# Hybrid decoder block on one core: the first sixteen ada_w blocks staged at once, the small constants issued by GpSimd

## The chip, the cores and the metric

The kernel runs on one core of a Trainium2 chip. The metric is the time of one execution in microseconds (us), as the device counts it; lower is better. Before the change the median of three runs is 2619.75 us.

## What is computed

One decoder layer over x (2048 tokens by 1024 features, float32). The parts that matter here stand at its start:

```python
c_act = jax.nn.silu(c)
ada = c_act @ ada_w[l] + ada_b[l]          # ada_w: 1024 x 6144
sh_a, sc_a, gt_a, sh_m, sc_m, gt_m = jnp.split(ada, 6)
h = rms_norm(x, pre_norm_mix[l]) * (1.0 + sc_a) + sh_a
y = hybrid_mixer(h, ...)                    # its first step is h @ w_in
x = x + gt_a * rms_norm(y, post_norm_mix[l])
h = rms_norm(x, pre_norm_mlp[l]) * (1.0 + sc_m) + sh_m
y = jnp.square(jax.nn.relu(h @ w_up[l])) @ w_down[l]
x = x + gt_m * rms_norm(y, post_norm_mlp[l])
```

The mixer joins four heads of chunked gated linear attention and four heads of rotary differential attention, and is followed by a squared-ReLU MLP. Nothing of h, and so nothing of the projections, can be formed before the scale `sc_a` and the shift `sh_a` are known.

## The kernel before

The kernel is one long program for the five engines and the DMA queues, written with pools and tiles. A scheduler orders each engine's instructions, and each engine then runs its own list strictly in that order. Matmul operands are split into a high and a low float32r half, so that a product is three matmuls. The program's stages are: the start (ada vectors, the first normalisation), the input projections and the gated linear attention, the differential attention, the output projection, the MLP.

The start goes like this. `ada_chunk(j)` (from L352) forms `c_act @ ada_w` for 1024 columns, number j of six: for each of the eight blocks of 128 rows, SyncE (SP) asks for a 128x1024 float32 block `adaraw` (512 KB, L357) and VectorE (DVE) multiplies it by a column of `ca` (the activated c) and adds it to `adacc`, at L359 for the first block and L361 for the other seven. The tile `adaraw` has the tag `wraw` with three buffers, so a fourth block is asked for when the first has been used. `ada_cols(j)` (L365) then sums `adacc` over its partitions with eight one-column matmuls by `ones` (L369, PSUM tile `adaps`), and L370 adds the sums to `cols`, which held the bias `ada_b`.

The top of the program (from L430) runs j=1 (the scale) for three blocks, then `load_consts()`, twelve small transfers issued by SP (L100 to L111), then the other five blocks. `make_a1` (L386) makes the multiplier `prem`. j=0 (the shift) follows in the same way; after its third block `load_x(0)` asks for the first 512 tokens of x, four tiles `nx` of 128x1024. `load_norm` squares each on ScalarE (ACT, L140, tile `njunk`, sums in `nss`), `rsqrt_col` (L120 to L129, tiles `nry`, `nrv`, `nrw`, `nrr`) makes the root, L145 scales the four tiles on ACT. `modulate` transposes them on TensorE (PE, L155, `ntr`), and ACT applies multiplier and shift at L157 (`nhf`); from these come the operands `hThi` and `hTlo` (L158, L160) of `hT[0]`. The low-rank gate (`lrps` L513 and L514, `zps` L519) and the projections (`projn`, L502 to L504) come next.

A DMA's landing is counted on a semaphore. SP's transfers go round eight of them, so a ninth is not issued before the first of the eight ahead of it has landed; GpSimd (POOL) has eight of its own.

Of the kernel before, what the change touches and what calls it, by code (L numbers as in the profile page):

```python
# [9 lines left out]
F32 = mybir.dt.float32  # L10
# [9 lines left out]
P = 128  # L20
S = 2048
D = 1024
NK = D // P
# [26 lines left out]
def tile_hybrid_block(  # L50
# [3 lines left out]
    nc = tc.nc  # L54
# [35 lines left out]
    cols = const.tile([P, 48], F32, name="cols")  # L90
    prem = const.tile([P, 2, NK], F32, name="prem")
    postm = const.tile([P, 2, NK], F32, name="postm")
    gnc = const.tile([P, 2], F32, name="gnc")
    gbc = const.tile([P, 2], F32, name="gbc")
    ivf = const.tile([P, 1], F32, name="ivf")
    gw2 = const.tile([32, 2, P], F32, name="gw2")
    lamt = const.tile([P, 4, 64], F32, name="lamt")

    def load_consts():
        nc.sync.dma_start(cols, ada_b)  # L100
        nc.sync.dma_start(prem[:, 0, :], pre_mix)
        nc.sync.dma_start(prem[:, 1, :], pre_mlp)
        nc.sync.dma_start(postm[:, 0, :], post_mix)
        nc.sync.dma_start(postm[:, 1, :], post_mlp)
        nc.sync.dma_start(gnc[:, 0:1], gla_norm)
        nc.sync.dma_start(gnc[:, 1:2], diff_norm)
        nc.sync.dma_start(gbc, gate_b)
        nc.sync.dma_start(ivf, inv_freq)
        nc.sync.dma_start(gw2[0:16], gate_w)
        nc.sync.dma_start(gw2[16:32], gate_w)  # L110
        nc.sync.dma_start(lamt, lams.partition_broadcast(P))  # L111

    neglam = const.tile([P, 1], F32, name="neglam")

# [17 lines left out]
    def load_norm(src, xp, slots, on_act=False):  # L132

        xts = []
        ss = xp.tile([P, 4], F32, tag="nss", name="nss", bufs=2)
        for i in range(4):
            xt = xp.tile([P, D], F32, tag=slots[i][0], name="nx", bufs=slots[i][1])
            nc.sync.dma_start(xt, src[i])
            junk = xp.tile([P, D], BF16, tag="njunk", name="njunk", bufs=1)
            nc.scalar.activation(junk, xt, AF.Square, accum_out=ss[:, i:i + 1])  # L140
            xts.append(xt)
        r = rsqrt_col(xp, ss, 4, 1.0 / D, "nr")
        for i in range(4):
            if on_act:
                nc.scalar.activation(xts[i], xts[i], AF.Copy, scale=r[:, i:i + 1])  # L145
            else:
                nc.vector.tensor_scalar(xts[i], xts[i], r[:, i:i + 1], None, op0=ALU.mult)
        return xts
# [157 lines left out]
    sb = c0.enter_context(tc.tile_pool(name="p0", bufs=2, side="left"))  # L306
    sg = cG.enter_context(tc.tile_pool(name="p0g", bufs=2, side="right"))
# [3 lines left out]
    def ps_proj(name):  # L311
        return pp.tile([P, 512], F32, tag="A", name=name, bufs=2)
# [36 lines left out]
            nc.gpsimd.dma_start(ropeS[t][1], sn)  # L349
        tc.keep_in_program_order(nc.scalar.preload_act_table_set("natural_log_exp_and_others"))  # L350

    def ada_chunk(j, acc=None):  # L352
        if acc is None:
            acc = sb.tile([P, D], F32, tag="adacc", name="adacc", bufs=1)
        for k in range(NK):
            raw = sb.tile([P, D], F32, tag="wraw", name="adaraw", bufs=3)
            nc.sync.dma_start(raw, ada_w[k * P:(k + 1) * P, j * D:(j + 1) * D])  # L357
            if k == 0:
                nc.vector.tensor_scalar(acc, raw, ca[:, 0:1], None, op0=ALU.mult)  # L359
            else:  # L360
                nc.vector.scalar_tensor_tensor(acc, raw, ca[:, k:k + 1], acc, op0=ALU.mult, op1=ALU.add)  # L361
            yield
        return acc

    def ada_cols(j, acc=None):  # L365
        acc = yield from ada_chunk(j, acc)
        ps = ps_proj("adaps")
        for b in range(NK):
            nc.tensor.matmul(ps[:, b:b + 1], acc[:, b * P:(b + 1) * P], ones[:, 0:1], start=True, stop=True)  # L369
        nc.vector.tensor_tensor(cols[:, j * NK:(j + 1) * NK], cols[:, j * NK:(j + 1) * NK], ps[:, 0:NK], op=ALU.add)  # L370
# [13 lines left out]
    def make_a1(i, j):  # L384

        nc.vector.scalar_tensor_tensor(prem[:, i, :], cols[:, j * NK:(j + 1) * NK], 1.0, prem[:, i, :],  # L386
                                       op0=ALU.add, op1=ALU.mult)
# [8 lines left out]
    def run(g, n=None):  # L396

        while n is None or n > 0:
            if next(g, run) is run:
                return False  # L400
            n = None if n is None else n - 1
        return True
# [4 lines left out]
    def load_x(t):  # L407
        return load_norm([x[t * 512 + i * P:t * 512 + (i + 1) * P, :] for i in range(4)], sg, NX[t % 2], t == 0)
# [18 lines left out]
            wlo += [wl[:, k, :] for k in range(4)]  # L427
        return whi, wlo

    sc_a = ada_cols(1)  # L430
    run(sc_a, 3)
    load_consts()
    run(sc_a)
    make_a1(0, 1)
    sh_a = ada_cols(0, sb.tile([P, 4, 256], F32, tag="whi", name="adacc", bufs=3).rearrange("p a b -> p (a b)"))
    run(sh_a, 3)
    xts = load_x(0)
    run(sh_a)
    norm_in(0, xts, "CBDCBDCB")

# [406 lines left out]
    for k in range(NK):  # L847
        run(at, WL)
        raw = sw.tile([P, D], F32, tag="wx", name="woraw", bufs=3)
# [197 lines left out]
    wraw = {}  # L1047
# [119 lines left out]
    for s, (g, c, wi, p) in enumerate(usteps):  # L1167
        i = WORD[wi]
# [22 lines left out]
        whi, wlo = wsp.pop((p, i))  # L1191
# [207 lines left out]
    for s in range(nd - TAIL):  # L1399
        if s + AHEAD < nd:  # L1400
            ready_ops[s + AHEAD] = down_ops(*dsteps[s + AHEAD])
        i, p, gs = dsteps[s]
# [98 lines left out]
```

## Time and profile before

| what | value |
|---|---|
| median of 3 runs | 2619.75 us (2618.13 to 2629.93) |
| the profiled execution's own time | 2620.44 us |
| its span, first to last instruction | 2618.7 us |
| granted TensorE clock, mean share of full | 0.982 |
| PE busy, by matmuls | 2482.6 us (95%) |
| DVE busy | 1595.4 us (61%) |
| ACT busy | 1154.8 us (44%) |
| POOL busy | 435.5 us (17%) |
| DMA moved | 491.63 MB, 188 GB/s on average |

Busy shares are averages over stages with different limits. The profile's times run from the first instruction of the span; 1.7 us of the execution's own time lie outside the span.

### The profile page before, as it was taken

The page shows a single profiled execution, that of the slowest core. Times are in us where ns is not written, and L with a number is a line of the kernel's source. Part 1 is how long each engine was busy: PE and PEld are TensorE (multiplying, and loading weights), DVE is VectorE, ACT ScalarE, POOL GpSimd, SP SyncE. Part 2 cuts the span into 40 slices and gives each one's busy share as a digit, 9 for nine tenths or more (in the row PEclk, how much of TensorE's full clock was granted, in tenths as well). Part 3 has the DMA queues.
Part 4 walks back from the last instruction along what each step waited for, and adds up shares of the span by engine and source line. Part 5 has one row for each costly group of instructions (what it writes and reads, how often), then busy time and mean ns, then how long its engine had stood idle before and what let it go on. Part 6 is the DMA issues. An engine that isn't in the chain of part 4 may idle for free.

```text
span 2618.7 us, 35437 instructions
## 1 busy us (share of the span) xinstructions
PE 2482.6 (95%) x12532; PEld 2043.2 (78%) x12532; DVE 1595.4 (61%) x3111; ACT 1154.8 (44%) x2185; POOL 435.5 (17%) x642
## 2 busy tenths in 40 slices
PE   3999999999998899999999999999999999999998
PEld 2887787987787787787877878788888888788886
DVE  5545765247764766766568666866665435443756
ACT  3351224323444655565546454655454324222444
POOL 1211332102320113223002231121121000100000
PEclk9999999999999899999999999999999999999999
DMA  6354552344744756565376564654447857755856
GB/s 235 107 193 137 170 196 77 125 131 155 224 155 142 227 173 207 186 201 187 109 261 234 194 238 141 225 190 144 139 151 258 289 189 234 268 197 162 282 168 208
DMA packets 219898, 491.63 MB, mean 188 GB/s; under 512 B 25872, under 2 KB 79936, under 8 KB 218176
## 3 DMA queue, kind: packets, MB, share of 16 engines
q1 hardware_dynamic: 171504, 329.33, 39.8%
q0 software_dynamic: 48208, 159.95, 16.3%
q8 instruction: 101, 1.65, 0.3%
q14 instruction: 85, 0.70, 0.1%
HBM read 329.79 MB, written 159.39 MB: 187 GB/s over the span
## 4 chain that ended last, share of the span: by engine, by line
PE 33%; issue 20%; DMA 5%; POOL 5%; DVE 3%; ACT 2%; SPq 0%; POOLq 0%; DVEq 0%; ACTq 0%
PE dn L1361 6%; PE dn L1363 6%; PE dn L1362 6%; PE O L252 3%; PE S L209 3%; PE Y L873 1%; PE Y L875 1%; POOL uS L1121 1%; PE Y L874 1%; POOL uS L1152 1%; PE PT L248 1%; DMA mx<-mixS 1%; PE upY L1195 1%; PE upY L1194 1%; PE upY L1193 1%
## 5 line engine op out<-in xcount | busy, mean ns | idle before, releaser
L1361 PE MATMUL dn<-dnhi,uhi 128*128 128x512 f32 x880 | 344.2, 391 | 4.8 <-DVE du L1339 4.7
L1363 PE MATMUL dn<-dnhi,ulo 128*128 128x512 f32 x880 | 343.8, 391 | 0.1
L1362 PE MATMUL dn<-dnlo,uhi 128*128 128x512 f32 x880 | 343.8, 391 | 0.0
L1285 ACT CAST uhi<-us 128x1024 fp32r<-128x1024 f32 (+1 forms) x126 | 118.7, 944 | 352.6 <-PE dn L1362 325.8
L1287 DVE TENSOR_TENSOR ulo<-us,uhi 128x1024 fp32r<-128x1024 f32 (+1 forms) x126 | 137.0, 1087 | 152.6 <-ACT uhi L1285 149.9
L209 PE MATMUL S<-K,q 128*128 128x512 f32 (+3 forms) x640 | 193.9, 402 | 14.2 <-DVE P L214 7.5
L488 PE MATMUL projt<-hThi,whi 128*128 128x512 f32 x512 | 206.3, 403 | 0.6 <-DVE cols L370 0.3
L489 PE MATMUL projt<-hTlo,whi 128*128 128x512 f32 x512 | 205.9, 402 | 0.0
L490 PE MATMUL projt<-hThi,wlo 128*128 128x512 f32 x512 | 201.8, 394 | 2.1 <-DVE wlo L425 2.1
L1361 PEld LDWEIGHTS dn<-dnhi,uhi 128*128 128x128 f32 x880 | 165.7, 188 | 41.0 <-issue 5.1
L1363 PEld LDWEIGHTS dn<-dnhi,ulo 128*128 128x128 f32 x880 | 165.7, 188 | 35.7 <-DVE ulo L1287 0.6
L1362 PEld LDWEIGHTS dn<-dnlo,uhi 128*128 128x128 f32 x880 | 165.7, 188 | 35.1
L227 ACT ACTIVATE P<-P,nm 128x128 f32<-128x128 f32 (+15 forms) x128 | 153.8, 1203 | 65.2 <-DVE nm L217 59.7
L1075 ACT CAST wuhi<-wA 128x512 fp32r<-128x512 f32 x160 | 99.1, 619 | 162.7 <-PE upV L1194 67.2
L252 PEld LDWEIGHTS O<-V,PTs 128*128 128x128 f32 x1088 | 136.5, 193 | 33.4 <-ACT PTs L250 26.6
L252 PE MATMUL O<-V,PTs 128*128 128x128 f32 x1088 | 154.7, 285 | 7.3 <-ACT PTs L250 3.5
L1195 PE MATMUL upY<-hhi,wulo 128*128 128x512 f32 x384 | 151.0, 393 | 1.5 <-DVE wulo L1076 1.5
L1193 PE MATMUL upY<-hhi,wuhi 128*128 128x512 f32 x384 | 150.9, 393 | 0.0
L1194 PE MATMUL upY<-hlo,wuhi 128*128 128x512 f32 x384 | 150.9, 393 | 0.0
L502 PE MATMUL projn<-whi,hThi 128*128 128x256 f32 x512 | 147.2, 288 | 3.8 <-DVE cols L370 2.3
L209 PEld LDWEIGHTS S<-K,q 128*128 128x128 f32 x640 | 111.7, 197 | 48.8 <-DVE P L214 21.9
L503 PE MATMUL projn<-wlo,hThi 128*128 128x256 f32 x512 | 146.7, 287 | 0.0
(321 smaller groups left out, 5759.9 us busy)
## 6 DMA issues: line engine op xcount, KB each, us to landing
us<-uS SPq DMA_DIRECT2D x94, 512.0 KB, 4.5
wA<-in_w_up_dram SPq DMA_DIRECT2D x128, 256.0 KB, 3.0
uS<-t POOLq DMA_DIRECT2D x128, 256.0 KB, 3.2
adaraw<-in_ada_w_dram SPq DMA_DIRECT2D x48, 512.0 KB, 4.4
wraw<-in_w_in_dram SPq DMA_DIRECT2D x48, 512.0 KB, 4.5
uS<-c POOLq DMA_DIRECT2D x96, 256.0 KB, 3.0
K<-kS SPq DMA_DIRECT2D x40, 512.0 KB, 4.6
wds<-in_w_down_dram SPq DMA_DIRECT2D x78, 256.0 KB, 4.3
```

What stands on the lines that cost most here:

```text
L209: nc.tensor.matmul(ps[:, :wd], qt[:, m, hl, qs], Kc[ci][:, m, :wd], start=(hl == 0), stop=(hl == 1))
L227: nc.scalar.activation(Ps[m][:, :width], Ps[m][:, :width], AF.Exp, scale=-1.0, bias=nms[m][:, t:t + 1], accum_out=sums[:, 0, m:m + 1])
L252: nc.tensor.matmul(outs[t, h][:, j, :], pt[:, kb % 4, :], Vc[g][:, kb % 4, :], start=(kb == 0), stop=(kb == nb - 1))
L488: nc.tensor.matmul(ps, whi[k][:, cs], hi[:, k, :], start=(k == 0), stop=False)
L489: nc.tensor.matmul(ps, whi[k][:, cs], lo[:, k, :], start=False, stop=False)
L490: nc.tensor.matmul(ps, wlo[k][:, cs], hi[:, k, :], start=False, stop=(k == NK - 1))
L1193: nc.tensor.matmul(ps, whi[:, k, :], hi[:, k, :], start=(first and k == 0), stop=False, skip_group_check=not first)
L1194: nc.tensor.matmul(ps, whi[:, k, :], lo[:, k, :], start=False, stop=False, skip_group_check=not first)
L1195: nc.tensor.matmul(ps, wlo[:, k, :], hi[:, k, :], start=False, stop=(k == 3), skip_group_check=not first)
L1361: nc.tensor.matmul(banks[t], uhi[:, tk], whi, start=first, stop=False, skip_group_check=on)
L1362: nc.tensor.matmul(banks[t], uhi[:, tk], wlo, start=False, stop=False, skip_group_check=on)
L1363: nc.tensor.matmul(banks[t], ulo[:, tk], whi, start=False, stop=last, skip_group_check=on)
```

## The change

Five edits go together. The twelve constants are issued by POOL instead of SP. A new `ada_stage(j)` asks for all eight blocks of one j at once, into tiles `adast` that take the buffers later used for `hThi` and `hTlo` (two buffers each, four blocks to a buffer). The order of SP's requests is then: eight blocks of j=1, the four tiles of x, eight blocks of j=0. `load_norm` is split, so that the normalisation of x is a function of its own, `norm_rows`, with the same operations. `ada_chunk` and `ada_cols` take the staged blocks, where there are any. The other four j are loaded as before.

```diff
     def load_consts():
-        nc.sync.dma_start(cols, ada_b)
-        nc.sync.dma_start(prem[:, 0, :], pre_mix)
...
-        nc.sync.dma_start(lamt, lams.partition_broadcast(P))
+        nc.gpsimd.dma_start(cols, ada_b)
+        nc.gpsimd.dma_start(prem[:, 0, :], pre_mix)
...
+        nc.gpsimd.dma_start(lamt, lams.partition_broadcast(P))
...
-    def ada_chunk(j, acc=None):
+    def ada_stage(j):
+
+        raws = []
+        for tag in ("hThi", "hTlo"):
+            st = sb.tile([P, NK, 512], F32, tag=tag, name="adast", bufs=2).rearrange("p (r a) b -> p r (a b)", a=2)
+            for r in range(4):
+                k = len(raws)
+                nc.sync.dma_start(st[:, r, :], ada_w[k * P:(k + 1) * P, j * D:(j + 1) * D])
+                raws.append(st[:, r, :])
+        return raws
+
+    def ada_chunk(j, acc=None, raws=None):
...
-            raw = sb.tile([P, D], F32, tag="wraw", name="adaraw", bufs=3)
-            nc.sync.dma_start(raw, ada_w[k * P:(k + 1) * P, j * D:(j + 1) * D])
+            if raws is None:
+                raw = sb.tile([P, D], F32, tag="wraw", name="adaraw", bufs=3)
+                nc.sync.dma_start(raw, ada_w[k * P:(k + 1) * P, j * D:(j + 1) * D])
+            else:
+                raw = raws[k]
...
-    sc_a = ada_cols(1)
-    run(sc_a, 3)
     load_consts()
-    run(sc_a)
+    sc_raw = ada_stage(1)
+    x0 = [sg.tile([P, D], F32, tag="nx", name="nx", bufs=4) for _ in range(4)]
+    for i in range(4):
+        nc.sync.dma_start(x0[i], x[i * P:(i + 1) * P, :])
+    sh_raw = ada_stage(0)
+    run(ada_cols(1, raws=sc_raw))
     make_a1(0, 1)
-    sh_a = ada_cols(0, sb.tile([P, 4, 256], F32, tag="whi", name="adacc", bufs=3).rearrange("p a b -> p (a b)"))
+    sh_a = ada_cols(0, sb.tile([P, 4, 256], F32, tag="whi", name="adacc", bufs=3).rearrange("p a b -> p (a b)"), sh_raw)
     run(sh_a, 3)
-    xts = load_x(0)
+    xts = norm_rows(x0, sg, True)
     run(sh_a)
     norm_in(0, xts, "CBDCBDCB")
```

On SP's queue before, from the second of the two `gnc` constants to the first loads of the input weights (`wraw`; `lraw` is the gate's weight):

```order
L106 DMA gnc<-in_diff_norm_dram 128x1
L107 DMA gbc<-in_gate_b_dram 128x2
L108 DMA ivf<-in_inv_freq_dram 128x1
L109 DMA gw_125<-in_gate_w_dram 16x256
L110 DMA gw_125<-in_gate_w_dram 16x256
L111 DMA lamt<-in_lams_dram 128x256
L357 DMA adaraw<-in_ada_w_dram 128x1024 x8
L138 DMA nx<-in_x_dram 128x1024 x4
L357 DMA adaraw<-in_ada_w_dram 128x1024 x5
```

Ahead of these stand `ccol` (the vector c), three blocks and the first six constants. On SP's queue now, from its start, with what each request waits for (DMAHW0 to DMAHW7 are the eight semaphores of SP's transfers):

```order
L89 DMA ccol<-in_c_dram 128x8
L363 DMA adast<-in_ada_w_dram 128x1024 x7
L363 DMA adast<-in_ada_w_dram 128x1024 [waits DMAHW0_49]
L452 DMA nx<-in_x_dram 128x1024 [waits DMAHW1_49]
L452 DMA nx<-in_x_dram 128x1024 [waits DMAHW2_49]
L452 DMA nx<-in_x_dram 128x1024 [waits DMAHW3_49]
L452 DMA nx<-in_x_dram 128x1024 [waits DMAHW4_49]
L363 DMA adast<-in_ada_w_dram 128x1024 [waits DMAHW5_49]
L363 DMA adast<-in_ada_w_dram 128x1024 [waits DMAHW6_49]
```

The constants are gone from between the blocks, the waits on DVE are gone too, and x stands behind eight blocks instead of eleven; six more blocks of j=0 follow the last row.

On DVE before, from the second block of j=1 to the root of x (`nrr`):

```order
L361 SCALAR_TENSOR_TENSOR adacc<-adaraw,ca,adacc 128x1024 x2
L472 TENSOR_SCALAR gnc<-gnc 128x1
L361 SCALAR_TENSOR_TENSOR adacc<-adaraw,ca,adacc 128x1024 x5
L370 TENSOR_TENSOR cols<-cols,adaps 128x8
L359 TENSOR_SCALAR adacc<-adaraw,ca 128x1024
L386 SCALAR_TENSOR_TENSOR prem<-cols,prem 128x8
L361 SCALAR_TENSOR_TENSOR adacc<-adaraw,ca,adacc 128x1024 x2
L123 TENSOR_SCALAR nrv<-nss 128x4
L361 SCALAR_TENSOR_TENSOR adacc<-adaraw,ca,adacc 128x1024
L126 TENSOR_TENSOR nrw<-nry 128x4
L127 SCALAR_TENSOR_TENSOR nrw<-nrw,nrv 128x4
L129 SCALAR_TENSOR_TENSOR nrr<-nrw,nry 128x4
```

And on DVE now, from the same place to the end of the shift's blocks:

```order
L379 SCALAR_TENSOR_TENSOR adacc<-adast,ca,adacc 128x1024 x5
L493 TENSOR_SCALAR gnc<-gnc 128x1
L379 SCALAR_TENSOR_TENSOR adacc<-adast,ca,adacc 128x1024 x2
L388 TENSOR_TENSOR cols<-cols,adaps 128x8
L404 SCALAR_TENSOR_TENSOR prem<-cols,prem 128x8
L123 TENSOR_SCALAR nrv<-nss 128x4
L377 TENSOR_SCALAR adacc<-adast,ca 128x1024
L126 TENSOR_TENSOR nrw<-nry 128x4
L127 SCALAR_TENSOR_TENSOR nrw<-nrw,nrv 128x4
L129 SCALAR_TENSOR_TENSOR nrr<-nrw,nry 128x4
L379 SCALAR_TENSOR_TENSOR adacc<-adast,ca,adacc 128x1024 x7
```

The scaling of a constant (`gnc`) moved behind six blocks of j=1, and all eight blocks of j=0 moved behind `nrv`, which needs all of x; before, three of them stood ahead of it. Past this place the lists of all engines hold the same operations in the same order, but for one swap of a transpose and a gate matmul on PE.

## Rows read from the trace of the kernel before

**Rows 1.** Busy time by stretch: span, PE, PEld, DVE, ACT, POOL, clock, DMA share, GB/s

```profile
0.00:65.36 65.36, 22.68 (x85) 14.65 (x85) 35.88 (x61) 22.03 (x34) 7.54 (x12) 0.92 0.69 235
400.00:2618.00 2218.00, 2145.13 (x10683) 1761.83 (x10682) 1365.47 (x2723) 1020.30 (x1922) 353.86 (x540) 0.99 0.57 190
```

**Rows 2.** Waits from 0 to 66 us: total, times, longest

```profile
PE adaps L369 <- DVE adacc L361: 25.4, 2, 24.0
...
DVE adacc L361 <- DMA adaraw<-in_ada_w_dram: 11.7, 6, 6.3
```

**Rows 3.** Timeline of SP, merged: start, time, instruction, count

```profile
1.25 1.37 SPq L357 DMA_DIRECT2D adaraw<-in_ada_w_dram  x3
...
10.60 13.68 SPq L357 DMA_DIRECT2D adaraw<-in_ada_w_dram  x8
24.33 1.91 SPq L138 DMA_DIRECT2D nx<-in_x_dram  x4
```

**Rows 4.** Timeline of DVE, with the idle time before and what ended it

```profile
5.44 0.75 DVE L359 TENSOR_SCALAR adacc<-adaraw,ca 128x1024 f32<-128x1024 f32 x1 [1.97 <-DMA adaraw<-in_ada_w_dram]
7.03 2.61 DVE L361 SCALAR_TENSOR_TENSOR adacc<-adaraw,ca,adacc 128x1024 f32<-128x1024 f32 x2 [0.84 <-DMA adaraw<-in_ada_w_dram]
...
16.04 3.93 DVE L361 SCALAR_TENSOR_TENSOR adacc<-adaraw,ca,adacc 128x1024 f32<-128x1024 f32 x3 [6.33 <-DMA adaraw<-in_ada_w_dram]
...
36.39 0.17 DVE L123 TENSOR_SCALAR nrv<-nss 128x4 f32<-128x4 f32 x1 [5.02 <-ACT njunk L140]
...
37.70 0.16 DVE L126 TENSOR_TENSOR nrw<-nry 128x4 f32<-128x4 f32 x1
...
38.17 2.60 DVE L361 SCALAR_TENSOR_TENSOR adacc<-adaraw,ca,adacc 128x1024 f32<-128x1024 f32 x2
...
44.86 1.28 DVE L361 SCALAR_TENSOR_TENSOR adacc<-adaraw,ca,adacc 128x1024 f32<-128x1024 f32 x1 [1.83 <-DMA adaraw<-in_ada_w_dram]
```

**Rows 5.** Timeline of ACT

```profile
32.66 1.06 ACT L140 ACTIVATE njunk<-nx 128x1024 bf16<-128x1024 f32 x1 [0.20 <-DMA nx<-in_x_dram]
...
35.21 1.06 ACT L140 ACTIVATE njunk<-nx 128x1024 bf16<-128x1024 f32 x1
...
38.29 4.27 ACT L145 ACTIVATE nx<-nx,nrr 128x1024 f32<-128x1024 f32 x4 [1.36 <-DVE nrr L129]
48.53 5.46 ACT L157 ACTIVATE nhf<-ntr,cols,prem 128x512 f32<-128x512 f32 x8 [5.97 <-DVE cols L370]
```

**Rows 6.** Timeline of PE

```profile
23.98 3.58 PE L369 MATMUL adaps<-ones,adacc 128*128 128x1 f32 x16 [23.98 <-DVE adacc L361]
39.58 5.24 PE L155 MATMUL ntr<-ident,nx 128*128 128x128 f32 x24 [12.03 <-ACT nx L145]
46.20 2.09 PE L369 MATMUL adaps<-ones,adacc 128*128 128x1 f32 x16 [1.38 <-DVE adacc L361]
...
65.36 0.58 PE L502 MATMUL projn<-whi,hThi 128*128 128x256 f32 x1
```

**Rows 7.** Stretches of two us, columns as in the first group

```profile
6.00:8.00 2.00, 0.00 (x0) 0.00 (x0) 1.16 (x2) 0.00 (x0) 0.00 (x0) 1.00 0.92 289
8.00:10.00 2.00, 0.00 (x0) 0.00 (x0) 1.66 (x3) 0.00 (x0) 0.00 (x0) 1.00 0.09 1
10.00:12.00 2.00, 0.00 (x0) 0.00 (x0) 0.00 (x0) 0.00 (x0) 0.00 (x0) 1.00 0.29 52
...
14.00:16.00 2.00, 0.00 (x0) 0.00 (x0) 0.00 (x0) 0.00 (x0) 0.00 (x0) 1.00 1.01 363
...
34.00:36.00 2.00, 0.00 (x0) 0.00 (x0) 0.00 (x0) 1.87 (x3) 0.00 (x0) 1.00 1.03 422
```

**Rows 8.** Timeline of POOL: two issues of a DMA

```profile
77.63 1.25 POOL L554 DMA_DIRECT2D gvS<-gvev  x1 [17.21 <-ACT gvev L553]
...
104.92 0.72 POOL L554 DMA_DIRECT2D gvS<-gvev  x1 [12.58 <-ACT gvev L553]
```

**Rows 9.** DMA issues from 180 to 200 us: count, KB each, us to landing

```profile
ropeS<-cn POOLq DMA_DIRECT2D x4, 256.0 KB, 5.6
```

More of the change, by code (lines that the diff above doesn't have):

```diff
@@ L99, in load_consts @@
     def load_consts():
-        nc.sync.dma_start(cols, ada_b)
-        nc.sync.dma_start(prem[:, 0, :], pre_mix)
[L102 to L110, printed above, removed]
-        nc.sync.dma_start(lamt, lams.partition_broadcast(P))
+        nc.gpsimd.dma_start(cols, ada_b)
+        nc.gpsimd.dma_start(prem[:, 0, :], pre_mix)
+        nc.gpsimd.dma_start(prem[:, 1, :], pre_mlp)
+        nc.gpsimd.dma_start(postm[:, 0, :], post_mix)
+        nc.gpsimd.dma_start(postm[:, 1, :], post_mlp)
+        nc.gpsimd.dma_start(gnc[:, 0:1], gla_norm)
+        nc.gpsimd.dma_start(gnc[:, 1:2], diff_norm)
+        nc.gpsimd.dma_start(gbc, gate_b)
+        nc.gpsimd.dma_start(ivf, inv_freq)
+        nc.gpsimd.dma_start(gw2[0:16], gate_w)
+        nc.gpsimd.dma_start(gw2[16:32], gate_w)
+        nc.gpsimd.dma_start(lamt, lams.partition_broadcast(P))
     neglam = const.tile([P, 1], F32, name="neglam")
@@ L134, in load_norm @@
         xts = []
-        ss = xp.tile([P, 4], F32, tag="nss", name="nss", bufs=2)
         for i in range(4):
@@ L138, in load_norm, with norm_rows @@
             nc.sync.dma_start(xt, src[i])
+            xts.append(xt)
+        return norm_rows(xts, xp, on_act)
+    def norm_rows(xts, xp, on_act):
+        ss = xp.tile([P, 4], F32, tag="nss", name="nss", bufs=2)
+        for i, xt in enumerate(xts):
             junk = xp.tile([P, D], BF16, tag="njunk", name="njunk", bufs=1)
             nc.scalar.activation(junk, xt, AF.Square, accum_out=ss[:, i:i + 1])
-            xts.append(xt)
         r = rsqrt_col(xp, ss, 4, 1.0 / D, "nr")
@@ L363, in ada_chunk, with ada_cols @@
         return acc
-    def ada_cols(j, acc=None):
-        acc = yield from ada_chunk(j, acc)
+    def ada_cols(j, acc=None, raws=None):
+        acc = yield from ada_chunk(j, acc, raws)
         ps = ps_proj("adaps")
```

## The prediction

> **What bounds the kernel now.** I read three views, from coarse to fine. First busy time by stretch [rows 1]: from 400 us on PE is busy 2145 of 2218 us, while in the first 65.36 us it is busy 22.68. The body is a PE-bound program; the start is not, and the reader is to see there how little PE does before its first projection. Then the waits of the start [rows 2]: PE's largest is for DVE's `adacc`, 25.4 us, and DVE in turn waited 11.7 us for blocks of ada_w. So the start is a chain: block lands, DVE adds it, PE sums the partitions, ACT applies scale and shift. Then the timelines, for who is late on that chain. SP asks for three blocks at 1.25 us and for the fourth at 10.60 [rows 3]; DVE, done with the third at 9.64, sits idle 6.33 us until the fourth has landed at 16.04 [rows 4]. Later it waits for x: `nrv` starts at 36.39 after 5.02 idle us, and the last block is added from 44.86 to 46.14. PE's sum of the shift takes 2.09 us [rows 6], ACT's first modulation starts at 48.53 [rows 5], and the first projection matmul at 65.36 [rows 6].
>
> All engines' lists past the start are the same before and after. So I price the change by one number, how much earlier the modulation at 48.53 starts, and then ask whether what follows keeps it.
>
> **Landing of the blocks.** The first three are asked for as before, so they land as before: 5.44, 7.03, and the third by 8.3, since DVE goes straight on to it [rows 4]. From then on up to eight requests are in flight, which before was nearly so only while x was loaded: from 34 to 36 us the DMAs moved 422 GB/s [rows 7], that is 524,288 bytes in 1.24 us, and ACT's squares from the second tile of x to the fourth, 32.66 to 35.21, follow the landings at 1.28 us each [rows 5]. I take 1.28. Block n of the new queue lands at 8.3 + 1.28 (n − 3): the eighth, the last of the scale, at 14.7; the twelfth, the last of x, at 19.8; the twentieth, the last of the shift, at 30.1.
>
> **The constants on POOL.** SP loses twelve issues; POOL gains them. One costs it 0.72 to 1.25 us [rows 8], so all are out between about 10 and 17 us after POOL's own start-up, and POOL's first work on data comes after the modulation: the issues themselves cost nothing. The transfers do not vanish, though. Before, they passed in stretches with little else: 0.09 and 0.29 of 2 us [rows 7], 0.76 us, and between 6 and 8 us, where the 578 KB moved (289 GB/s) would need 1.37 us at 422 GB/s and the DMAs were busy 1.84, another 0.47. That is 1.2 us of the DMAs' time, which now falls between the blocks. No row shows descriptors of a few bytes written by GpSimd; I bound this delay by 0 and by twice 1.2, and take 1.2. So x is complete at 21.0 and the last shift block at 31.3. The Trainium skill's page "DMA: Bandwidth & Descriptors", section "Issuing engines are not separate DMA queues", says that transfers from all issuing engines run on the same 16 DMA engines and interleave, and that a second issuing engine saves only sequencer time. By that rule the 1.2 us stays in the sum; if the constants moved on a path of their own, the sum would be 1.2 us shorter. POOL's stores beside a loaded SP queue took 5.6 us to land [rows 9], so they did share, and were not held until it was empty.
>
> **DVE's chain now.** Its adds run at 3.93/3 = 1.31 us [rows 4]. The scale: the second block at 7.03, seven adds, 9.2 us, done at 16.2, or about 17.4 with the constants' delay. In the middle DVE scales `gnc`, after five adds (13.6): the second `gnc` is POOL's seventh issue, out by 6.8 to 10.5 and landed some 3 to 5.6 us later, so it could hold DVE by 2 us at most. PE's sum of the scale takes 3.58 us as before [rows 6], so `cols` and `prem` are done near 21.5. Next on DVE is `nrv`, which needs the square of x's last tile: from 35.21 to 36.39 it took 1.18 us [rows 4, 5], so 22.2. The scale and any wait for `gnc` thus have about 0.7 us to spare; beyond that they cost one for one. Then the shift: the first block's multiply takes the place of an add between `nrv` and `nrw`, which were 1.31 apart [rows 4]; the multiply is 0.54 shorter, so `nrw` is near 23.0, and the first add 0.47 later, 23.5. Seven adds at 1.31 end at 32.7. The last block, landed at 31.3 and then 1.28 to add, would give 32.6: DVE and the DMAs are even here. Against 46.14 that is **13.4 us earlier**.
>
> **PE's sum of the shift.** Before, it followed the transposes by 1.38 us and took 2.09; the sum of the scale, after 24 us of idle PE, took 3.58 [rows 6]. Now ACT scales x from 23.6, and the transposes end 6.5 us after ACT's start (38.29 to 44.82), at 30.1, so PE idles 2.6 us before the sum. Between 2.09 and 3.58 I take 2.8, a loss of 0.7. The modulation starts at 32.7 + 0.05 + 2.8 + 0.25 = 35.8 instead of 48.53: **12.7 us earlier**.
>
> **What follows.** From 48.53 to 65.36 the chain is ACT, DVE, POOL and PE on data in SBUF. The gate weight and the first two weight blocks now stand right behind the shift, and land by 8.3 + 1.28 × 20 + 1.2 = 35.1, eleven us before their casts are due. The next 512 tokens' x and the third weight block come after; the fourth waits for a buffer that DVE frees, which moves with the rest. Nothing there holds the gain back, so it lasts to the end, as PE has little idle time past 400 us [rows 1] and no work is added or taken away. The waits that leave: 6.33 us of DVE for the fourth block and the late x. What is late next is DVE's own adds.
>
> Sum, against the profiled execution: 2620.44 − 12.7 = 2607.7. The median of the runs is 0.69 us below that execution, so I predict **2607.0 us**.
>
> **Rivals.** *The DMAs do not keep the pace of 34 to 36 us.* With three blocks outstanding they were just as busy from 14 to 16 us, but moved 363 GB/s [rows 7], or 1.44 us a block. Then x is complete at 8.3 + 9 × 1.44 + 1.2 = 22.5 and the last block at 34.0, added at 35.3: 10.8 less 0.7 makes 10.1 us, 2609.6. For it: twenty blocks in a row have no row. Against: 422 GB/s with a fuller queue. The Trainium skill's same page, section "Where 436 GB/s comes from", says that for loads from HBM the limit of about 358 GB/s binds. By that rule the time would be this rival's; the trace is above it from 34 to 36 us, so I give it little.
>
> *More than the sum.* The constants hide (0 instead of 1.2) and PE's sum stays at 2.09: 13.4 + 1.2 = 14.6, 2605.2. Against: two lucky ends at once. Stretches of low clock before the first projections may also fall otherwise.
>
> *The constants starve.* If POOL's transfers get no turn until SP's queue is empty, `gnc` lands only after 27 requests of about block size (twenty blocks, two weights, four tiles of x, the gate weight): 8.3 + 1.28 × 23 = 37.7. DVE stands before it with two adds of the scale undone: 40.3, the sum 43.9, `prem` 44.4, the shift's eight blocks 10.5 later, 54.9, and the modulation at 58 instead of 48.53. That is 9.5 us slower, 2629. It decides from the point where `gnc` lands later than some 28 us; up to 14 or so it costs nothing. For it: DVE's list has `gnc` in the middle of the scale. Against: POOL's stores landed beside SP's loads [rows 9].
>
> *The gain is given back.* A wait in the projections that I don't see takes half of it: 2613. Against: same order, same buffers, earlier data.
>
> **How the numbers follow.** Forecast 0.60, slow DMAs 0.15, more than the sum 0.15, starvation 0.04, given back 0.06. The forecast's own range comes from the constants' bounds (14.6 − 2.4 to 14.6, before PE's sum) and PE's loss (0 to 1.5): gains of 10.7 to 14.6, so 2605 to 2609. I take 2602 to 2614: it holds the slow DMAs, the richer case and half given back, and leaves out the starved case and what I have not thought of. About 0.5%, 13.1 us, is what a measurement of this kernel can tell from no change; the forecast lies just short of it. Faster by more: the richer case and some 0.4 of the forecast, 0.40. Slower by more: a starved case worse than priced, 0.03. The rest, 0.57, is within.
>
> **What would show it.** In the new profile: blocks landing 1.25 to 1.3 us apart from the third on; DVE with no idle time of several us between 7 and 17 us; `nrv` near 22, the last shift add ending near 32.7, the modulation near 35.8, the first projection near 52.6, and everything after shifted by the same amount. It is wrong if `gnc` or `prem` waits for a DMA of POOL, if the blocks land 1.4 us or more apart, or if the shift at 52.6 has shrunk by the attention.

## The result and the profile after

Beside the kernel before on one chip, the changed kernel took 2606.85 us (median of 8 runs, 2599.92 to 2612.56) and the kernel before 2622.89 us (8 runs, 2618.13 to 2629.93): a ratio of 0.9937, 95% interval 0.9921 to 0.9953. The profiled execution of the changed kernel took 2606.38 us with a span of 2604.7 us, against 2620.44 and 2618.7 before; the granted clock is 0.982 of full in both. Two later measurements, on two different chips, gave ratios of 0.9955 (0.994 to 0.997) and 0.9949 (0.9933 to 0.9965). The kernel is faster by about 0.5%, some 14 us.

Busy time by stretch, columns as in [rows 1]; the first two lines answer to those rows, the stretches of two us to [rows 7], and the last two are used further down.

```profile
0.00:53.69 53.69, 23.37 (x85) 15.63 (x85) 36.14 (x61) 22.04 (x34) 14.21 (x24) 0.88 0.76 286
400.00:2604.00 2204.00, 2133.03 (x10591) 1750.73 (x10589) 1357.56 (x2716) 1013.26 (x1913) 350.40 (x537) 0.99 0.58 191
...
6.00:8.00 2.00, 0.00 (x0) 0.00 (x0) 1.05 (x2) 0.00 (x0) 0.81 (x2) 1.00 1.06 397
8.00:10.00 2.00, 0.00 (x0) 0.00 (x0) 1.68 (x2) 0.00 (x0) 1.31 (x3) 1.00 1.00 304
10.00:12.00 2.00, 0.00 (x0) 0.00 (x0) 1.34 (x2) 0.00 (x0) 0.28 (x1) 1.00 0.99 363
...
18.00:20.00 2.00, 2.00 (x11) 2.00 (x11) 0.00 (x0) 1.80 (x4) 0.00 (x0) 1.00 1.02 408
...
26.00:28.00 2.00, 2.00 (x10) 1.63 (x10) 1.96 (x2) 2.00 (x3) 0.00 (x0) 1.00 1.02 408
...
33.34:36.41 3.07, 3.07 (x16) 2.98 (x16) 0.41 (x3) 0.00 (x0) 0.00 (x0) 0.59 1.04 414
...
830.00:900.00 70.00, 53.25 (x282) 41.79 (x282) 46.26 (x134) 39.90 (x86) 9.82 (x14) 0.88 0.73 230
```

The start holds the same work (PE 23.37 us now, 22.68 before, DVE 36.14 and 35.88) in 53.69 us instead of 65.36: 11.67 us went out of the idle time. POOL's 14.21 us instead of 7.54 are its twelve issues. The hole in the DMAs is gone: from 8 to 10 us they move 304 GB/s, where before it was 1. They are not at their full pace yet, with 304 and 363 GB/s up to 12 us against 408 from 18 us on, after the last constant has landed at 15.62.

The waits of the start, to be held against [rows 2] (us in total, times, longest):

```profile
PE adaps L387 <- DVE adacc L379: 20.4, 2, 17.8
...
DVE adacc L379 <- DMA adast<-in_ada_w_dram: 2.4, 6, 0.9
DVE adacc L377 <- DMA adast<-in_ada_w_dram: 1.9, 1, 1.9
```

The adds of DVE waited 11.7 us for blocks; now they wait 2.4, six times, never more than 0.95, and those 2.4 us are a hint that the blocks of the scale do not come at full pace. SP's queue shows why the long wait left (start, time, instruction, count; [rows 3] before):

```profile
1.25 4.39 SPq L363 DMA_DIRECT2D adast<-in_ada_w_dram  x8
5.68 4.86 SPq L452 DMA_DIRECT2D nx<-in_x_dram  x4
11.87 9.92 SPq L363 DMA_DIRECT2D adast<-in_ada_w_dram  x8
```

All eight blocks are asked for by 5.64 us, where the fourth was asked for at 10.60 before. DVE's timeline ([rows 4]):

```profile
5.41 0.75 DVE L377 TENSOR_SCALAR adacc<-adast,ca 128x1024 f32<-128x1024 f32 x1 [1.93 <-DMA adast<-in_ada_w_dram]
7.11 1.29 DVE L379 SCALAR_TENSOR_TENSOR adacc<-adast,ca,adacc 128x1024 f32<-128x1024 f32 x1 [0.95 <-DMA adast<-in_ada_w_dram]
8.63 1.28 DVE L379 SCALAR_TENSOR_TENSOR adacc<-adast,ca,adacc 128x1024 f32<-128x1024 f32 x1 [0.23 <-DMA adast<-in_ada_w_dram]
10.29 1.28 DVE L379 SCALAR_TENSOR_TENSOR adacc<-adast,ca,adacc 128x1024 f32<-128x1024 f32 x1 [0.38 <-DMA adast<-in_ada_w_dram]
...
14.68 0.15 DVE L493 TENSOR_SCALAR gnc<-gnc 128x1 f32<-128x1 f32 x1
...
16.42 1.28 DVE L379 SCALAR_TENSOR_TENSOR adacc<-adast,ca,adacc 128x1024 f32<-128x1024 f32 x1 [0.17 <-DMA adast<-in_ada_w_dram]
21.37 0.16 DVE L388 TENSOR_TENSOR cols<-cols,adaps 128x8 f32<-128x8 f32 x1 [3.66 <-PE adaps L387]
21.57 0.17 DVE L404 SCALAR_TENSOR_TENSOR prem<-cols,prem 128x8 f32<-128x8 f32 x1
22.71 0.17 DVE L123 TENSOR_SCALAR nrv<-nss 128x4 f32<-128x4 f32 x1 [0.98 <-ACT njunk L145]
...
24.04 9.25 DVE L379 SCALAR_TENSOR_TENSOR adacc<-adast,ca,adacc 128x1024 f32<-128x1024 f32 x7
```

The scale ends at 17.70, `nrv` starts at 22.71 instead of 36.39, and the shift's adds run without a gap until 33.29, where they ended at 46.14. ACT and PE ([rows 5] and [rows 6]):

```profile
21.53 1.06 ACT L145 ACTIVATE njunk<-nx 128x1024 bf16<-128x1024 f32 x1
...
36.64 5.46 ACT L161 ACTIVATE nhf<-ntr,cols,prem 128x512 f32<-128x512 f32 x8 [8.34 <-DVE cols L388]
```

```profile
17.76 3.57 PE L387 MATMUL adaps<-ones,adacc 128*128 128x1 f32 x16 [17.76 <-DVE adacc L379]
25.33 5.39 PE L159 MATMUL ntr<-ident,nx 128*128 128x128 f32 x24 [4.00 <-ACT nx L149]
33.34 3.07 PE L387 MATMUL adaps<-ones,adacc 128*128 128x1 f32 x16 [2.62 <-DVE adacc L379]
...
53.69 0.58 PE L523 MATMUL projn<-whi,hThi 128*128 128x256 f32 x1
```

The modulation starts at 36.64 instead of 48.53, 11.89 us earlier, and the first projection at 53.69 instead of 65.36. POOL's timeline shows the issues that [rows 8] could only suggest:

```profile
5.01 0.54 POOL L106 DMA_DIRECT2D gnc<-in_diff_norm_dram  x1
5.54 0.74 POOL L107 DMA_DIRECT2D gbc<-in_gate_b_dram  x1
7.47 0.53 POOL L108 DMA_DIRECT2D ivf<-in_inv_freq_dram  x1 [1.19 <-DMA cols<-in_ada_b_dram]
```

The second `gnc`, on which the rival of the starved constants hung, was issued at 5.01 and landed at 10.73, 4 us before DVE scales it. After eight issues POOL waits 1.19 us for the first to land; nobody waits for that.

### The profile page after: what moved, and what is told of

Same layout as the page of the kernel before. It is cut to its first block, busy times and chain, and to the rows that moved or that the text cites. A ratio compares the mean times of both kernels' runs of the same rounds, so it can differ in the third digit from the quotient of the medians.

```text
span 2604.7 us, 35436 instructions
## 1 busy us (share of the span) xinstructions
PE 2482.8 (95%) x12532; PEld 2043.7 (78%) x12532; DVE 1593.4 (61%) x3111; ACT 1154.1 (44%) x2185; POOL 440.8 (17%) x654
## 4 chain that ended last, share of the span: by engine, by line
PE 37%; issue 20%; POOL 3%; DMA 3%; DVE 2%; ACT 2%; POOLq 0%; DVEq 0%; SPq 0%; ACTq 0%
PE dn L1382 4%; PE dn L1383 4%; PE dn L1384 4%; PE upY L1216 2%; PE upY L1214 2%; PE upY L1215 2%; PE O L256 2%; PE S L213 2%; PE upX L1216 2%; PE upV L1214 2%; PE upV L1216 2%; PE upV L1215 2%; PE upX L1214 2%; PE upX L1215 2%; PE PT L252 1%
```

## The experiments

Each kernel was timed on one chip, beside runs of the kernel before on the same chip. The start is read from each profile by two marks, the first modulation on ACT and the first projection matmul on PE; "the rest" is the span less the second mark.

| kernel | time, us | ratio to before (95%) | modulation | projection | rest |
|---|---|---|---|---|---|
| before, first profile | 2622.89 | 1 | 48.53 | 65.36 | 2553.3 |
| before, again | 2617.89 | 0.9997 (0.9982 to 1.0012) | 48.92 | 65.96 | 2550.2 |
| changed, first | 2606.85 | 0.9937 (0.9921 to 0.9953) | 36.64 | 53.69 | 2551.0 |
| changed, second | 2607.92 | 0.9955 (0.9940 to 0.9970) | 37.66 | 54.50 | 2547.5 |
| changed, third | 2606.40 | 0.9949 (0.9933 to 0.9965) | 36.55 | 53.59 | 2556.1 |
| constants on SP | 2613.02 | 0.9970 (0.9958 to 0.9981) | 42.24 | 58.72 | 2549.6 |
| constants on POOL alone | 2617.13 | 0.9987 (0.9976 to 0.9998) | 44.02 | 60.27 | 2551.1 |
| x first | 2612.71 | 0.9969 (0.9957 to 0.9982) | 41.19 | 58.25 | 2553.7 |
| constants late | 2605.40 | 0.9944 (0.9927 to 0.9962) | 34.56 | 54.35 | 2555.7 |
| shift in halves | 2606.27 | 0.9948 (0.9930 to 0.9966) | 32.15, 41.73 | 54.65 | 2549.0 |
| halves, constants late | 2606.79 | 0.9946 (0.9930 to 0.9961) | 30.03, 39.78 | 55.14 | 2549.4 |
| gate weight first | 2607.67 | 0.9952 (0.9936 to 0.9968) | 35.39 | 52.23 | 2551.7 |

The next four kernels were timed together on one chip, where the kernel before had a median of 2621.49 us in 33 runs.

**Both kernels again.** After the first result the question was whether the 16 us between the two medians are more than the start's 11.7. The kernel before was run unchanged:

> The kernel before, unchanged, for a second profile. The theory: the change moves the start alone (first modulation 48.5 to 36.6 us, first projection 65.4 to 53.7), and what stands behind the first projection (2553.3 us in the profile before, 2551.0 in the one after) is the same work whose time differs from run to run by some us with the low-clock stretches. So here: first projection within 0.5 us of 65.4, and a rest of 2549 to 2560. The rival, that some 4 us of the 16 between the medians are won behind the start: a rest of 2555 or more here, and of 2551 or less in every profile of the changed kernel.

Its ratio to itself is 0.9997, so that a ratio from ten runs is good to about 0.0015, 4 us. The rest is 2550.2 us, as the theory had it and not the rival's 2555 or more, and the first projection comes at 65.96, a little outside its half microsecond. And the changed kernel, unchanged:

> The changed kernel, unchanged, for a second profile and more times. The theory: first projection within 0.5 us of 53.7, a rest between 2547 and 2560 us, and a gain over the kernel before that comes nearer to 12 us as runs are added (ratio 0.9945 to 0.9960). The rival: a rest of 2551 or less and a gain that stays at 16 (ratio 0.9939 or lower).

The ratio is 0.9955, or 11.8 us: the 16 us did not come again, and the theory of the start alone holds here. In this profile the fourth block of the scale landed at 10.83 instead of 10.20 and PE's sum of the shift took 3.58 us, so the modulation is 1.0 us later than in the first, and the projection, at 54.50, is 0.8 later, where half a microsecond was expected.

**Undoing the move of the constants.**

```diff
     def load_consts():
-        nc.gpsimd.dma_start(cols, ada_b)
...
-        nc.gpsimd.dma_start(lamt, lams.partition_broadcast(P))
+        nc.sync.dma_start(cols, ada_b)
...
+        nc.sync.dma_start(lamt, lams.partition_broadcast(P))
```

> The changed kernel with the twelve constants issued by SP again, ahead of the staged blocks (nothing on POOL). The theory, that the start is a chain from the blocks' landing: SP's twelve issues of 0.45 us put off the first block by 5.5 us, and the blocks then land 1.28 us apart without the constants between them, so the modulation starts near 40 us instead of 36.6, and the time is 3 to 4 us above the changed kernel, about 2610. The rival, that the constants leaving SP are the whole gain: most of the 12 us is lost, 2617 to 2619.

DVE's timeline of this kernel, the first block and the seven adds of the scale:

```profile
12.72 0.75 DVE L377 TENSOR_SCALAR adacc<-adast,ca 128x1024 f32<-128x1024 f32 x1 [6.41 <-DMA adast<-in_ada_w_dram]
13.97 9.21 DVE L379 SCALAR_TENSOR_TENSOR adacc<-adast,ca,adacc 128x1024 f32<-128x1024 f32 x7 [0.50 <-DMA adast<-in_ada_w_dram]
```

The first block is added 7.31 us later than in the changed kernel, not the 5.5 that were expected: it is asked for 5.67 us later, behind twelve issues, and takes 5.70 us to land instead of 4.06. But then the blocks land 1.25 to 1.29 us apart from the very first (the last after 1.32), and the last of the shift at 36.95, only 5.2 us after the changed kernel's 31.77. The modulation, at 42.24 instead of near 40, is 5.60 us later than in the changed kernel and 6.3 earlier than before; the time is 2613.02 us, where about 2610 was expected, and the ratio is 0.9970. The rival, that the constants leaving SP are the whole gain, falls.

**The move of the constants alone**, in the kernel before, without the staging.

```diff
+    load_consts()
     sc_a = ada_cols(1)
-    run(sc_a, 3)
-    load_consts()
     run(sc_a)
```

with `load_consts` as the change has it.

> The kernel before with the twelve constants issued by POOL and nothing staged: three buffers for ada_w as before. The theory: the idle time of 6.3 us before the fourth block goes, the blocks still land 1.5 us and more apart, as each waits for a buffer, and x comes as late as ever behind them; modulation near 43 us, gain 5 to 6 us, about 2617. The rival, that the constants are the whole gain: modulation near 37 us, gain 12 us.

DVE's timeline, the fourth and the fifth block of the scale, and `nrv`:

```profile
11.23 1.28 DVE L361 SCALAR_TENSOR_TENSOR adacc<-adaraw,ca,adacc 128x1024 f32<-128x1024 f32 x1 [1.47 <-DMA adaraw<-in_ada_w_dram]
14.22 1.28 DVE L361 SCALAR_TENSOR_TENSOR adacc<-adaraw,ca,adacc 128x1024 f32<-128x1024 f32 x1 [1.71 <-DMA adaraw<-in_ada_w_dram]
...
31.99 0.17 DVE L123 TENSOR_SCALAR nrv<-nss 128x4 f32<-128x4 f32 x1 [4.24 <-ACT njunk L140]
```

The hole of 6.33 us before the fourth block is down to 1.47, but with three buffers a block is asked for only when DVE has done with an old one, and waits of 0.3 to 1.8 us stay, as does the late x. The modulation starts at 44.02, 4.51 us earlier than before, about as the theory had it (near 43, 5 to 6 us); the ratio is 0.9987, and the rival falls. By the marks the two parts give 4.5 and 6.3 us alone and 11.9 together: they add up, with 1.1 us to spare. Neither is for nothing, and the staging is the larger. The 6.3 holds for constants that SP issues ahead of all blocks; the last experiments put ten of them behind.

The next four were timed together on another chip (the kernel before: 2621.8 us, 18 runs).

**x ahead of the scale.** The change left x behind eight blocks; does it matter where it stands?

```diff
     load_consts()
-    sc_raw = ada_stage(1)
     x0 = [sg.tile([P, D], F32, tag="nx", name="nx", bufs=4) for _ in range(4)]
     for i in range(4):
         nc.sync.dma_start(x0[i], x[i * P:(i + 1) * P, :])
+    sc_raw = ada_stage(1)
     sh_raw = ada_stage(0)
```

> The changed kernel with x asked for ahead of all sixteen blocks. The theory, that the start is the chain of DVE in its listed order: the last of twenty requests lands as late as before (31.8 us), but on DVE's list the sum of the scale now stands between the two chunks, so DVE idles 3.6 us for PE between about 22.8 and 26.4, and then adds the shift for 9.9: modulation near 40 us instead of 36.6 to 37.7, 2 to 4 us above the changed kernel. The rival, that the DMAs alone set the end: modulation within 0.5 us of 36.6 to 37.7, as the twentieth request lands no later.

DVE's timeline, `cols` of the scale and the shift's seven adds:

```profile
27.25 0.16 DVE L388 TENSOR_TENSOR cols<-cols,adaps 128x8 f32<-128x8 f32 x1 [3.67 <-PE adaps L387]
...
28.12 9.21 DVE L379 SCALAR_TENSOR_TENSOR adacc<-adast,ca,adacc 128x1024 f32<-128x1024 f32 x7
```

The last block lands at 32.33, only 0.56 us later than in the changed kernel, but DVE has sixteen blocks of work behind x and stands idle 3.67 us in the middle of them, waiting for PE's sum, by whose end four blocks of the shift have landed (23.32 to 27.16). In the changed kernel the same wait passes while x lands (17.61 to 21.45). The shift's adds start 4.1 us later than in the changed kernel and end at 37.33, five us behind the last landing, and the modulation is 4.55 later, at 41.19, where near 40 was expected. So the start is the chain of DVE in its listed order, as the theory had it; the rival, that the DMAs alone set the end, falls.

**The constants behind the blocks.** Only `cols` and the first `prem`, needed first, stay on POOL; ten constants are asked for by SP behind the sixteen blocks.

```diff
         nc.gpsimd.dma_start(prem[:, 0, :], pre_mix)
-        nc.gpsimd.dma_start(prem[:, 1, :], pre_mlp)
...
+    def load_rest():
+        nc.sync.dma_start(prem[:, 1, :], pre_mlp)
...
     sh_raw = ada_stage(0)
+    load_rest()
```

> The changed kernel with only the two constants that are needed early (ada_b and the first gain) on POOL; the other ten are issued by SP behind the sixteen blocks. The theory, that the constants take the DMAs' time from the blocks (2.1 us by the landing of the twelfth request, 16.1 us after the first here against 14.1 with the constants gone): x complete near 19.8 instead of 21.5, modulation near 35 instead of 36.6 to 37.7, 1.5 to 2.5 us below the changed kernel. The rival, that the first blocks land 1.5 to 1.7 us apart because the DMAs start up slowly: no change, twelfth request again at 21.5.

DVE's timeline from the third block, with the adds of the shift and a cast of the gate's weight:

```profile
8.45 7.89 DVE L381 SCALAR_TENSOR_TENSOR adacc<-adast,ca,adacc 128x1024 f32<-128x1024 f32 x6 [0.19 <-DMA adast<-in_ada_w_dram]
...
22.46 9.25 DVE L381 SCALAR_TENSOR_TENSOR adacc<-adast,ca,adacc 128x1024 f32<-128x1024 f32 x7
...
44.08 0.28 DVE L473 TENSOR_TENSOR lw<-lraw,lw 128x128 fp32r<-128x128 f32 x1
```

The stretch from 8 to 10 us (columns as in [rows 1]), where the changed kernel moved 304 GB/s:

```profile
8.00:10.00 2.00, 0.00 (x0) 0.00 (x0) 1.77 (x3) 0.00 (x0) 0.00 (x0) 1.00 1.04 416
```

Without the ten constants between them the blocks land 1.27 to 1.29 us apart from the third on (the last after 1.33), the last at 30.17 instead of 31.77: what the ten cost in the changed kernel is 1.60 us by these two profiles. By all profiles it is 1.4 to 2.3, since the last block lands at 31.77, 32.25 and 31.60 in the three of the changed kernel and at 30.17 and, in the last kernel below, 29.94 without them. The rival of a slow start of the DMAs falls. The modulation starts at 34.56, 2.1 us earlier. But the first projection, at 54.35, is not earlier. The waits of this kernel name the place:

```profile
PE lrps L537 <- DVE lw L473: 7.1, 1, 7.1
```

The gate's weight `lraw` stands behind ten constants on SP and lands at 34.75 instead of 31.95. DVE's list, which the scheduler made anew for this order, has its casts among those of the modulated x (the last at 44.08, where the changed kernel had done all by 33.75), and PE stands before the gate's first matmul for 7.1 us. The 2 us won were given back 10 us later. This is the rival "the gain is given back" of the prediction, made by hand.

**The shift in column halves**, so that half of the modulation can start after half of the blocks' bytes.

```diff
-    sh_raw = ada_stage(0)
+    sh_raw = ada_stage_halves(0)
...
-    sh_a = ada_cols(0, sb.tile([P, 4, 256], F32, tag="whi", name="adacc", bufs=3).rearrange("p a b -> p (a b)"), sh_raw)
+    sh_a = ada_cols_halves(0, sb.tile([P, 4, 256], F32, tag="whi", name="adacc", bufs=3).rearrange("p a b -> p (a b)"), sh_raw)
```

The new functions load and add eight blocks of 128x512 for the left half, sum them with eight matmuls, and then do the same for the right half.

> The changed kernel with the shift's blocks asked for, added and summed by column halves (eight blocks of 128x512 for the first 512 columns, then eight for the others), so that the first four of the eight modulations start before the second half has landed. The theory, that the end of the start is the chain last block, add, PE's sum, modulation, operands: the first modulation starts near 30 us, the fifth near 35, the first projection 4 to 7 us earlier than 53.7 to 54.5, and the time is 4 to 7 us below the changed kernel, about 2601. The rival, that DVE is the bound from 24 us on and the casts of the first half only push its adds back: first projection less than 2 us earlier.

ACT's timeline:

```profile
32.15 2.79 ACT L161 ACTIVATE nhf<-ntr,cols,prem 128x512 f32<-128x512 f32 x4 [2.12 <-PE ntr L159]
41.73 2.79 ACT L161 ACTIVATE nhf<-ntr,cols,prem 128x512 f32<-128x512 f32 x4 [5.86 <-DVE cols L390]
```

The first four modulations start 4.5 us earlier, the other four 2.4 us later than the changed kernel's fifth (39.3, at 0.67 each from 36.64). DVE's casts of the first half push its adds of the second half apart (33.30, 34.57, 35.57, 36.57, 38.84; between 30.85 and 39.91 it idles once, for 0.57 us), and PE waits for them:

```profile
PE adaps L388 <- DVE adacc L384: 3.7, 1, 3.7
```

So it came as the rival said and not as the theory: DVE is the bound up to the second sum, the first projection starts at 54.65 instead of 4 to 7 us earlier, and the time is that of the changed kernel. The halves are not shown to be worthless by it. PE's list has the gate's first matmul behind the second sum, at 42.22, and DVE's has the casts of the gate's weight there too; another order of the lists was not tried.

**Halves with the constants late**: the edits of the last two together.

> Both of the last two: column halves for the shift, and ten constants behind the blocks. The theory: the two gains add, first projection 6 to 9 us earlier than in the changed kernel, 2598 to 2601. The rival: with halves DVE is the bound, and the constants' place no longer shows, so no more than with halves alone.

The first modulation comes at 30.03, the fifth at 39.78, the first projection at 55.14. The theory of 6 to 9 us missed: the earliest modulation of all goes with a projection later than the changed kernel's. PE's waits show what lies between the two marks:

```profile
PE lrps L562 <- DVE lw L498: 6.6, 1, 6.6
```

It is the wait of the kernel with the late constants: `lraw` lands at 36.17 behind the ten constants, and PE stands before the gate's first matmul until DVE has cast it. So this kernel does not tell what the halves are worth with the constants late.

The last two kernels were timed together on a third chip (the kernel before: 2619.84 us, 13 runs).

**The gate's weight ahead of the late constants.** The wait that took the gain in the kernel with the late constants is removed by asking for `lraw` first:

```diff
     sh_raw = ada_stage(0)
+    lraw0 = sb.tile([P, NK, 16], F32, tag="wraw", name="lraw", bufs=3)
+    nc.sync.dma_start(lraw0, w_lr)
     load_rest()
...
-    glac = gla_consts(sg, sb.tile([P, NK, 16], F32, tag="wraw", name="lraw", bufs=3))
+    glac = gla_consts(sg, lraw0, False)
```

> The changed kernel with only `cols` and the first `prem` on POOL; the gate's weight `lraw` is asked for right behind the sixteen blocks, and the ten other constants behind it, all by SP. This is the late-constants kernel with the one request that cost it its gain moved ahead of the constants. Theory (the start is a chain of landings, and the constants belong where nothing waits): blocks 1.28 us apart, last one near 30.2, `lraw` landed near 30.4, DVE casts it before the modulation as in the changed kernel (near 31.7 to 32.3), the modulation starts at 34.6 and the first projection matmul at 51.5 to 52.2, 1.5 to 2.2 us before the changed kernel's 53.69; the time is about 2 us below the changed kernel's on the same chip, near 2605, less than the medians can tell apart by themselves. Rival (another bound sits between the modulation and the projections, such as the gate's chain through `gw` or the first two `wraw`, which land some 2 us later than in the changed kernel): the modulation starts at 34.6, but the first projection stays between 53.4 and 54.5, and the time is that of the changed kernel.

PE's timeline, the sum of the shift and the first projection:

```profile
31.58 3.57 PE L389 MATMUL adaps<-ones,adacc 128*128 128x1 f32 x16 [3.13 <-DVE adacc L381]
...
52.23 0.58 PE L529 MATMUL projn<-whi,hThi 128*128 128x256 f32 x1
```

DVE's casts of the gate's weight stand at 31.44, ahead of the modulation again, PE's wait for `lw` is gone, and the first projection comes at 52.23, 1.36 to 2.27 us before the changed kernel's three profiles and the earliest of all. It follows the modulation by 16.84 us, as in the changed kernel (16.84 to 17.05), where it was 19.79 with the wait. So the wait for `lw` was the cause, and the rival of another bound between the marks falls. The modulation is later than the theory had it (35.39, not 34.6), because PE's sum took 3.57 us this time. In the runs nothing of it can be told: 2607.67 us beside the changed kernel's 2606.40 on the same chip, where 2 us less was expected, and a ratio of 0.9952, among the changed kernel's own three. It also shows that POOL is not what the gain hangs on: ten of the twelve constants are back on SP here, and both marks are earlier than with POOL issuing them beside the blocks.

**The changed kernel, a third time**, on that chip:

> The changed kernel again, beside the kernel above on the same chip. Theory (the start alone, about 12 us): modulation between 36 and 38 us, first projection between 53.5 and 54.7, time 11 to 13 us below the kernel before (ratio 0.995 to 0.9958). Rival (the 16 us between the first medians hold, 4 of them from behind the start): 15 us or more, ratio 0.9943 or less.

The marks came as the theory had them, 36.55 and 53.59; the ratio, 0.9949 or 13.4 us, lies between the two theories.

**What the runs say together.** The rest behind the first projection took 2553.3 and 2550.2 us in the two profiles of the kernel before, and 2551.0, 2547.5 and 2556.1 in three of the changed one: means of 2551.8 and 2551.5. No gain and no loss is seen there, only a scatter of up to 8.6 us between executions of the same program. An example of how one place differs is the stretch from 830 to 900 us, which stands above for the first profile of the changed kernel (clock 0.88, PE busy 53.25 us). In its second profile:

```profile
830.00:900.00 70.00, 55.34 (x313) 44.12 (x312) 49.99 (x139) 42.43 (x89) 9.83 (x14) 0.93 0.78 254
```

The granted clock is 0.93 there, and 0.93 in the third profile too, which has the longest rest; so this stretch alone does not set the scatter. Against that scatter the times go as the marks do: those with the projection at 58 to 60 us have ratios of 0.9969 to 0.9987, and the seven with it at 52 to 55 us of 0.9937 to 0.9955. The mean of the changed kernel's three ratios is 0.9947, 13.9 us, some 2 us above the start's 11.7; each interval is 4 us to either side, and where those 2 us would come from, if they are real, stays open.

## Why the prediction was right

The time was forecast as 2607.0 us and came out at 2606.85; the profiled execution as 2607.7 and it took 2606.38. The mechanism is the one that was forecast, and most steps came within a microsecond. By the prediction's steps:

- **Landing of the blocks.** The pace of 1.28 us a block held over x and the shift, twelve in a row, but not over the scale. X and the shift's blocks landed at 17.61, 18.89, 20.17, 21.45 and on to 31.77, and the two-us stretches from 18 to 28 us show 406 to 414 GB/s. From the third block to the eighth, though, the scale's landed 1.45 to 1.67 us apart, as DVE's adds at 8.63, 10.29, 11.95, 13.48, 14.97 and 16.42 show. That is a sign that the prediction had named for being wrong (1.4 us or more apart). The kernel with the late constants decides between the two readings: without the ten constants the same blocks land 1.28 us apart, so it was the constants' delay, spread over five blocks, and not a slower pace of the DMAs. The rival of the slow DMAs, 1.44 us a block throughout, falls. The Trainium skill's page "DMA: Bandwidth & Descriptors", section "Where 436 GB/s comes from", says that for loads from HBM a limit of about 358 GB/s binds, and names beside it a load of 16 MB measured at 425 GB/s. The trace does not agree with the limit, with 408 GB/s from 18 to 20 and from 26 to 28 us, and the measurement decides.
- **The constants on POOL.** The issues cost nothing, as forecast: 0.50 to 0.74 us each, the last done at 10.28. The transfers cost more than the 1.2 us taken: the formula without them puts the eighth, twelfth and twentieth request at 14.7, 19.8 and 30.1, and they landed at 16.33, 21.45 and 31.77, 1.6 to 1.7 late. The kernel with the late constants gives 1.60 for ten of them. This term was mis-sized, by 0.4 us and within its bounds. The estimate stopped counting at 12 us, while `lamt`, the largest constant (128 KB of 0.21 MB), landed only at 14.66 in the kernel before. It also counted the DMAs' busy time of the constants alone: in the changed kernel their packets take 8.2% of the sixteen engines' time from 5 to 17 us, 0.98 us, and the rest of the 1.6 is what they take from the pace of the large transfers beside them (from 8 to 10 us 304 GB/s at a busy share of 1.00, against 416 at 1.04 with the constants late). The Trainium skill's sentence cited there, that the DMAs of all issuing engines run on the same DMA engines and interleave (same page, "Issuing engines are not separate DMA queues"), agrees with the trace: the constants on POOL's queue delayed the blocks on SP's by 1.6 us.
- **DVE's chain.** The scale was done at 17.70 (17.4 forecast), `prem` at 21.7 (21.5), `nrv` started at 22.71 (22.2), the shift's adds at 24.04 (23.5) and ended at 33.29 (32.7). The half microsecond is x's, which was complete at 21.45 instead of 21.0. The scale had 0.98 us to spare before `nrv`, where 0.7 was forecast, and DVE did not wait for `gnc`. "DVE and the DMAs are even here" held: the last block landed at 31.77, and its add ended at 33.29.
- **PE's sum of the shift.** PE idled 2.62 us (2.6 forecast) and the sum took 3.07 (2.8). The value was a guess between two rows, and the experiments show what sets it (below).
- **The modulation.** 11.9 us earlier, not 12.7: 0.6 from DVE's end and 0.27 from PE's sum. The first projection is 11.7 earlier, at 53.69 instead of 52.6.
- **What follows.** It keeps the gain, within the scatter of the rest. That the sum was 0.8 us too rich and the time still 0.15 us lower than forecast is luck. The forecast was counted from a median of 2619.75 us before, and beside the changed kernel the kernel before took 2622.89, so the gain by these medians was 16.0 us and not 12.7. The medians of the kernel before range from 2617.89 to 2622.89 us, and the marks say 11.7 to 11.9.
- **The rivals.** Starved constants: fell, `gnc` landed at 10.73. Gain given back: not in this kernel, though the late constants show that a wait of 7.1 us was one request's place away. More than the sum: its two lucky ends did not come; the constants cost more, and so did the sum.
- **The 0.5% border.** The forecast lay just short of it, and the three ratios, 0.45 to 0.63% below 1, lie on both sides of it.

## What to carry to other kernels

Where a PE-bound kernel begins with a chain of loads and adds, count how many requests are outstanding at each time: buffers that are needed only later can be lent to the start, and here the loads then ran back to back and the adds were even with them. Put the requests in the order in which their users need them (the constants were cheapest behind the blocks), and follow a moved request through every queue it passes: ten small constants placed ahead of one weight of 64 KB turned 2 us of gain into a wait of 7.1. When a gain is half a percent, read it from marks in the trace as well as from medians, since the same program scattered by 8 us behind those marks.

## What was not expected of the hardware

The length of PE's sum of the shift, sixteen matmuls of one column, is set by the granted clock. The same stretch in the profile of the constants on POOL alone (columns as above; PE had idled 1.19 us before it):

```profile
41.84:43.79 1.95, 1.94 (x16) 1.86 (x16) 0.41 (x3) 0.00 (x0) 0.00 (x0) 1.00 0.65 208
```

In the second profile of the changed kernel (idle for 3.25 us before):

```profile
33.85:37.43 3.58, 3.58 (x16) 3.49 (x16) 0.41 (x3) 0.00 (x0) 0.00 (x0) 0.50 1.02 404
```

It takes 1.95 us at 2.4 GHz, 3.58 at 1.2 GHz, and in the first profile of the changed kernel 3.07 at a mean of 0.59, since the clock fell at 33.92, half a microsecond into the sum. The idle time of PE before the sum orders all ten profiles in which it is sixteen matmuls: 0.87, 1.19, 1.38, 2.53, 2.62, 2.65, 2.81, 3.13, 3.25 and 10.16 us went with sums of 1.95, 1.95, 2.09, 2.55, 3.07, 3.14, 3.45, 3.57, 3.58 and 3.58. No run sets that idle time by itself, so this is an order and not yet a law. The kernel before, with 1.38 us of idle PE, had the shorter sum of 2.09, so 1.0 us of what DVE's earlier end brought was paid here.

The other is the price of the small constants. POOL's twelve are 0.21 MB in 400 packets, and ten of them delayed the blocks by 1.6 us. All twelve on SP ahead of the blocks put the first block 7.31 us and the last 5.2 us behind those of the changed kernel.
